# Index scores of a sparse attention: one whole pass and paired half-height matmuls in place of two whole passes

## The chip, the core and the metric

The kernel runs on one core of a Trainium2 chip. The metric is the device time of one execution in microseconds. TensorE (PE) multiplies matrices: each matmul has a weight load of its own (PEld) that can run ahead of it, and sums into one of eight banks of PSUM. ScalarE (ACT), VectorE (DVE) and GpSimd (POOL) work on tiles, and nearly all transfers are issued by SyncE's queue (SP), in its order.

## The reference, cut to what matters

A transformer block on 2048 tokens of width 1024: a first projection, an RWKV-7 branch, a branch of sparse attention, gates, output projections and a norm. The sparse attention chooses for each query its 256 best keys by an index score, and this score is what the change touches:

```python
qi = qi.reshape(B, S, IDX_HEADS, IDX_HEAD_DIM)          # 8 heads of 64
s_idx = jax.nn.relu(jnp.einsum('bqhd,bsd->bqhs', qi_b, ki))
score = jnp.einsum('bqh,bqhs->bqs', wi_b, s_idx).astype(jnp.float32)
score = jnp.where(causal[None], score, -jnp.inf)
_, sel = lax.top_k(score, topk)                         # topk = 256
```

All heads share one key `ki` of 64 numbers a token. Since a choice hangs on the scores, they are computed with operands split in two: a number is the sum of a "hi" part, rounded to the type float32r that TensorE multiplies in one pass, and a "lo" part, the rest.

## The kernel before, in words

`gemm_index` (lines 277 to 299) projects the index keys and queries for all tokens. `split_out` makes the hi and lo tiles of a projected tile ("eo" tiles, a pool of four); the keys go to the DRAM tensor `KIH` (hi and lo), the queries through `stacked` (lines 269 to 275) to `QIS`, where each head has 128 rows: 64 rows of hi and under them 64 of lo. That takes four DMAs of 128 KB for each of 16 projected tiles.

`select` (lines 372 to 496) works on blocks of 128 queries, blocks 2 to 15, in five groups of two or three blocks. For each block a tile `st` of 128 x 8 x 128 is loaded from `QIS` (line 412). The keys lie in SBUF in two tiles: `M[0]` holds the hi part twice, once in each half of the 128 rows, and `M[1]` the lo part twice. Keys up to the end of the block are taken in chunks of up to 512. For each chunk and each of 8 heads, two matmuls of 128 rows sum into a PSUM tile "ixs" (lines 418 and 419): the first gives hi by hi and lo by hi, the second hi by lo and lo by lo. ScalarE takes the relu into a tile "re" (line 421, three buffers), and VectorE adds it, weighted by the head, to the block's scores (line 425 or 427). After a group's scores come passes that seek a threshold (lines 440 to 467) and the mask (488 to 496).

```python
p = ps.tile([128, 512], FT, name="ixs")
T.matmul(p[:, :kn], st[:, h], M[0][:, k0:k0 + kn], start=True, stop=False)
T.matmul(p[:, :kn], st[:, h], M[1][:, k0:k0 + kn], start=False, stop=True)
r = w.tile([128, 512], FT, name="re", bufs=3)
A.activation(r[:, :kn], p[:, :kn], AF.Relu)
```

The pool of "ixs" tiles has six PSUM banks; the two others belong to the projection GEMM (tile "g", line 251), which goes on during the selection: `gemm_half` projects tokens 0 to 1023 for all other columns, 24 matmuls of 512 columns a tile. Its weights are loaded at line 230 and split at lines 236 and 237, and its results are stored from "eo" tiles at lines 340 and 349. A scheduler puts every engine's instructions in order beforehand, by a simulated timeline and by priorities (`band`): the selection has 20000 and the first half's projection 40000, and the lower number goes first where both are ready. After that come the second half's projection in 256-column matmuls, the RWKV-7 stage, the attention and the output projections.

In the RWKV-7 stage there are matmuls over fewer than 128 rows, which the prediction uses: in `rwkv_pass`, line 653 is a matmul over all rows, line 654 one over rows 64 to 127 and line 669 one over 40 rows from row 0, all of 512 columns in float32r.

Of the kernel before, what the change touches and what calls it, by code (L numbers as in the profile page):

```python
# [36 lines left out]
TB = 512  # L37
# [8 lines left out]
# first columns of the projections  # L46
# [5 lines left out]
class Block:  # L52
# [19 lines left out]
    def move(self, dst, src, q=None):  # L72
        """a DMA of float32r words as they are"""
        f = [a.bitcast(FT) if a.dtype == FR else a for a in (dst, src)]
        return (q or self.nc.sync).dma_start(f[0], f[1])
# [4 lines left out]
    # ---------------------------------------------------------------- constants  # L80
    def consts(self):
# [6 lines left out]
        # scratch in DRAM  # L88
        self.QIS = d.tile([8, 128, S], FR, name="qis")
# [22 lines left out]
    # ---------------------------------------------------------------- start: modulation, norm, h^T  # L112
    def start(self):
# [59 lines left out]
        # the last third of the modulation is for the end  # L173
# [9 lines left out]
        # bias by distance; beyond the last bucket's start it is constant and drops out of the softmax  # L183
# [12 lines left out]
    def ada(self, w, cT, j, ahead):  # L196
        """a third of the modulation, partial sums by partition"""
# [15 lines left out]
    # ---------------------------------------------------------------- the projection GEMM  # L213
    @contextmanager
    def urgent(self):
        """what frees or feeds the tensor engine goes before all else"""
        p = self.tc.cur_priority
        self.tc.cur_priority = self.hot
        yield
        self.hot = self.tc.cur_priority  # L220
        self.tc.cur_priority = p
# [33 lines left out]
    def split_out(self, p, scale=None, rows=128):  # L255
        """FR hi and lo of a PSUM tile."""
# [20 lines left out]
    def gemm_index(self):  # L277
# [5 lines left out]
        for tb in range(NTB):  # L283
# [11 lines left out]
            self.stacked(self.QIS, self.unit(qi, tb), 0, tb)  # L295
        for m in range(1, 4):
            wt = self.weights(C_QI + m * 128, 128)
            for tb in range(NTB):
                self.stacked(self.QIS, self.unit(wt, tb), m, tb)

    def gemm_half(self, tbs, kinds):
# [13 lines left out]
        # at the turn of the halves, a block of tokens serves two columns at a time  # L315
# [55 lines left out]
    # ---------------------------------------------------------------- index scores and the selection  # L371
    def select(self):
        """For each query the mask of its TOPK best keys (ties go to the lower index).

        A threshold is sought by the secant method on the count of scores at or above it, until the count is
        at most eight short of TOPK; the missing ones are then the largest below the threshold. Where the
        search has not ended so, a branch finds the TOPK-th largest value bit by bit.
        """
# [3 lines left out]
        with ExitStack() as ctx:  # L382
            k1 = self.pool("ix1", 1, side="right", ctx=ctx)
            w = self.pool("ixw", 2, side="right", ctx=ctx)
            ps = self.pool("ixp", 6, PSUM, ctx=ctx)
            M = [k1.tile([128, S], FR, name=f"kim{i}") for i in range(2)]
            for i in range(2):
                for r in range(2):
                    self.move(M[i][r * 64:r * 64 + 64], self.KIH[i])
# [8 lines left out]
            for grp in self.groups:  # L398
# [9 lines left out]
                for g, qb in enumerate(grp):  # L408
                    n, n1 = 128 * (qb + 1), 128 * qb
                    st = w.tile([128, 8, 128], FR, name="st")  # L410
                    self.move(st, self.QIS[:, :, qb * 128:(qb + 1) * 128].rearrange("h p q -> p h q"))
                    sco = w.tile([128, S], FT, name="sc", bufs=6)
                    sc.append(sco)
                    for k0 in range(0, n, 512):
                        kn = min(512, n - k0)
                        for h in range(8):
                            p = ps.tile([128, 512], FT, name="ixs")
                            T.matmul(p[:, :kn], st[:, h], M[0][:, k0:k0 + kn], start=True, stop=False)  # L418
                            T.matmul(p[:, :kn], st[:, h], M[1][:, k0:k0 + kn], start=False, stop=True)
# [9 lines left out]
                    # a first guess from mean and mean deviation of the keys that all rows see  # L429
# [10 lines left out]
                for it in range(self.passes):  # L440
                    if it:
                        # next threshold: a step of nothing once the count is near enough
# [15 lines left out]
                    for g, qb in enumerate(grp):  # L458
                        n = 128 * (qb + 1)
                        tg, cg = t[:, g:g + 1], cnt[:, g:g + 1]  # L460
                        if qb in self.on_act and it < self.passes - 1:
                            # with Sign a score equal to the threshold counts half: good enough to go on
# [5 lines left out]
                # rows that found their threshold  # L468
# [29 lines left out]
    def select_bits(self, grp, sc, hs, t, cnt, y, eq, w):  # L498
        """The selection for any scores: the TOPK-th largest value bit by bit, ties by prefix sums.

        Leaves 1 for the selected and 0 for the others as scores, and their threshold."""
# [24 lines left out]
    # ---------------------------------------------------------------- RWKV-7, chunks of 64  # L526
    def rwkv_open(self, ctx):
# [23 lines left out]
        # the small second factors: hi twice, and lo  # L551
# [48 lines left out]
    def parts(self, pool, t):  # L600
        """FR hi and lo of a tile"""
# [115 lines left out]
    def rwkv_inv(self, tb):  # L717
        """inverses of the unit triangular 32-blocks, one block a partition"""
# [23 lines left out]
    def rwkv_chain(self, tb):  # L742
# [8 lines left out]
        for c in range(8):  # L751
# [15 lines left out]
            # off-diagonal block of the inverse  # L767
# [51 lines left out]
    def chain_out(self, tb, half, yt, yvar):  # L819
        """group norm and bonus of half a block, with features on partitions"""  # L820
# [21 lines left out]
    # ---------------------------------------------------------------- keys and values of all heads  # L842
# [42 lines left out]
    # ---------------------------------------------------------------- attention over the selected keys  # L885
    def attention(self):
        nc, tc, x, d = self.nc, self.tc, self.x, self.d
        V, A, T, G, DMA = nc.vector, nc.scalar, nc.tensor, nc.gpsimd, nc.sync
        with ExitStack() as ctx:
# [7 lines left out]
            for h in range(8):  # L897
# [18 lines left out]
                for j in range(NQB // 2):  # L916
                    L = []
                    for qb in (2 * j, 2 * j + 1):
                        if h == 0:
                            # masks  # L920
# [66 lines left out]
    # ---------------------------------------------------------------- gates, output projections, last norm  # L987
    def split_weights(self, W, k1, w, names, eng, wide=D, **kw):
        """FR hi and lo of a matrix"""
# [15 lines left out]
    def gated(self, w, ps, fb, br, li=None, at=None, lb="lb"):  # L1005
        """a branch times silu of its gate, hi and lo"""
# [351 lines left out]
```

## Time and profile before

| | us |
|---|---|
| median of 3 runs | 2612.31 |
| lowest and highest run | 2610.18 and 2612.83 |
| span of the profiled execution | 2605.7 |
| TensorE busy in it | 2449.8 |
| VectorE busy in it | 1750.5 |

The span goes from the first to the last instruction of one profiled execution; what lies around it is not in the trace, and no separate time of that execution is listed. The matmuls' ends are modelled, so the distance from one matmul's start to the next one's says more than a duration. "Idle before" names what an engine waited for; "issue" means that the profile shows nothing.

### The profile page before, as it was taken

The page shows a single profiled execution, that of the slowest core. Times are in us where ns is not written, and L with a number is a line of the kernel's source. Part 1 is how long each engine was busy: PE and PEld are TensorE (multiplying, and loading weights), DVE is VectorE, ACT ScalarE, POOL GpSimd, SP SyncE. Part 2 cuts the span into 40 slices and gives each one's busy share as a digit, 9 for nine tenths or more (in the row PEclk, how much of TensorE's full clock was granted, in tenths as well). Part 3 has the DMA queues.
Part 4 walks back from the last instruction along what each step waited for, and adds up shares of the span by engine and source line. Part 5 has one row for each costly group of instructions (what it writes and reads, how often), then busy time and mean ns, then how long its engine had stood idle before and what let it go on. Part 6 is the DMA issues. An engine that isn't in the chain of part 4 may idle for free. (4 is left out here: it accounts for less than half of the span.)

```text
span 2605.7 us, 45357 instructions
## 1 busy us (share of the span) xinstructions
PE 2449.8 (94%) x16776; PEld 2153.8 (83%) x16776; DVE 1750.5 (67%) x3509; ACT 1229.8 (47%) x2136; POOL 868.2 (33%) x707
## 2 busy tenths in 40 slices
PE   4899999989899999899999999999989999999998
PEld 3687777868677899689898888988978999988887
DVE  6615888798988355774956947533468888877443
ACT  4315636446344423324334233343367888865332
POOL 2311131241323333223233322131155545645342
PEclk9999999999999999899999999999999999999999
DMA  7754222522233756568677669977763334145442
GB/s 245 271 149 127 77 85 73 131 77 88 84 103 102 243 162 202 147 192 234 179 219 204 187 189 284 293 233 189 239 199 116 91 88 118 45 152 195 147 150 77
DMA packets 423499, 415.69 MB, mean 160 GB/s; under 512 B 80010, under 2 KB 339890, under 8 KB 418404
## 3 DMA queue, kind: packets, MB, share of 16 engines
q1 hardware_dynamic: 422692, 404.33, 51.7%
q0 software_dynamic: 576, 8.39, 0.8%
q8 instruction: 132, 2.16, 0.4%
q14 instruction: 99, 0.81, 0.1%
HBM read 254.04 MB, written 160.15 MB: 159 GB/s over the span
## 5 line engine op out<-in xcount | busy, mean ns | idle before, releaser
L251 PE MATMUL g<-hh,whi 128*128 128x256 f32 (+1 forms) x2176 | 726.9, 334 | 14.8 <-DVE eo L265 4.5
L251 PE MATMUL g<-hl,whi 128*128 128x256 f32 (+1 forms) x2176 | 722.5, 332 | 3.9 <-POOL hl L169 2.4
L251 PE MATMUL g<-hh,wlo 128*128 128x256 f32 (+1 forms) x2176 | 721.0, 331 | 1.2 <-POOL wlo L237 1.2
L251 PEld LDWEIGHTS g<-hh,whi 128*128 128x128 f32 x2176 | 421.4, 194 | 63.8 <-issue 5.7
L251 PEld LDWEIGHTS g<-hl,whi 128*128 128x128 f32 x2176 | 421.0, 193 | 47.6 <-issue 3.9
L251 PEld LDWEIGHTS g<-hh,wlo 128*128 128x128 f32 x2176 | 420.7, 193 | 42.7 <-issue 3.9
L237 POOL TENSOR_TENSOR wlo<-wraw,whi 128x1024 fp32r<-128x1024 f32 (+1 forms) x89 | 216.9, 2437 | 629.4 <-ACT whi L236 583.0
L421 ACT ACTIVATE re<-ixs 128x512 f32<-128x512 f32 (+3 forms) x304 | 158.9, 548 | 176.1 <-DVE sc L427 109.8
L427 DVE SCALAR_TENSOR_TENSOR sc<-re,wi,sc 128x512 f32<-128x512 f32 (+3 forms) x266 | 222.6, 842 | 21.7 <-ACT re L421 6.5
L236 ACT CAST whi<-wraw 128x1024 fp32r<-128x1024 f32 (+1 forms) x89 | 92.8, 1042 | 175.1 <-PE g L251 131.0
L957 PE MATMUL pt<-ident,lt 128*128 128x128 f32 x1088 | 168.2, 276 | 6.4 <-ACT tp L963 3.5
L947 ACT ACTIVATE lt<-lt,nm 128x128 f32<-128x128 f32 (+15 forms) x128 | 154.7, 1211 | 14.2 <-DVE nm L946 14.1
L943 DVE CUSTOM_DVE_ANT_0 lt<-lg,mask 128x512 f32<-128x512 f32 (+3 forms) x256 | 147.4, 590 | 15.9 <-PE lg L941 7.5
L974 PE MATMUL yv<-ph,vp 128*128 128x256 f32 (+1 forms) x576 | 151.5, 285 | 6.7 <-ACT yl L978 4.7
L968 DVE TENSOR_TENSOR pl<-pt,ph 128x512 fp32r<-128x512 f32 (+1 forms) x216 | 139.1, 657 | 25.7 <-ACT ph L967 24.6
L974 PE MATMUL yv<-pl,vp 128*128 128x256 f32 x576 | 152.4, 300 | 2.0 <-POOL pl L965 2.0
L418 PE MATMUL ixs<-kim,st 128*128 128x512 f32 (+3 forms) x304 | 117.3, 387 | 28.7 <-ACT re L421 24.8
L940 PE MATMUL lg<-m,sq 128*128 128x256 f32 (+3 forms) x384 | 137.2, 366 | 5.0 <-DVE cm L943 4.1
L957 PEld LDWEIGHTS pt<-ident,lt 128*128 128x128 f32 x1088 | 125.9, 141 | 15.6 <-ACT tp L963 4.5
L941 PE MATMUL lg<-m,sq 128*128 128x256 f32 (+3 forms) x384 | 127.4, 337 | 0.0
L733 DVE TENSOR_TENSOR prd<-tm,ln 128x1 f32<-128x1 f32 (+30 forms) x124 | 113.3, 914 | 20.5 <-DMA pk<-pj 14.6
L967 ACT CAST ph<-pt 128x512 fp32r<-128x512 f32 (+1 forms) x216 | 115.9, 565 | 19.7 <-PE pt L957 13.7
(347 smaller groups left out, 5391.4 us busy)
## 6 DMA issues: line engine op xcount, KB each, us to landing
wraw<-in_w_in_dram SPq DMA_DIRECT2D x88, 512.0 KB
gg<-eo SPq DMA_DIRECT2D x64, 256.0 KB
gmd<-gt SPq DMA_DIRECT2D x64, 256.0 KB
gmc<-gmd SPq DMA_DIRECT2D x32, 512.0 KB
g<-gg SPq DMA_DIRECT2D x64, 256.0 KB
m<-ks SPq DMA_DIRECT2D x32, 512.0 KB
pj<-eo SPq DMA_DIRECT2D x52, 256.0 KB
x<-in_ada_w_dram SPq DMA_DIRECT2D x24, 512.0 KB
```

Source lines behind the costliest of these rows:

```text
L237: nc.gpsimd.tensor_tensor(lo[:, :, :n], raw[:, :, :n], hi[:, :, :n].bitcast(FT), op=OP.subtract)
L251: T.matmul(p[:, s], a[:, k], b[:, k, s], start=n == 0, stop=n == 3 * KD - 1)
L418: T.matmul(p[:, :kn], st[:, h], M[0][:, k0:k0 + kn], start=True, stop=False)
L421: A.activation(r[:, :kn], p[:, :kn], AF.Relu)
L427: V.scalar_tensor_tensor(o, r[:, :kn], wi, o, op0=OP.mult, op1=OP.add)
L940: T.matmul(p[:, :kn], sq[:, qb * 128:(qb + 1) * 128], m1[:, k0:k1_], start=True, stop=False)
L941: T.matmul(p[:, :kn], sq[:, qb * 128:(qb + 1) * 128], m2[:, k0:k1_], start=False, stop=True)
L943: V.tensor_tensor_reduce(lt[:, k0:k1_], p[:, :kn], mk, 1.0, -3.0e38, OP.add, OP.max, cm[:, i:i + 1])
L947: ex = A.activation(lt[:, :n], lt[:, :n], AF.Exp, bias=nm, accum_out=lsum[:, qb, h:h + 1])
L957: T.transpose(p[:, o:o + 128], L[i][:, kt * 128:(kt + 1) * 128], self.ident)
L968: V.tensor_tensor(pl[:, :n], p[:, :n], ph[:, :n].bitcast(FT), op=OP.subtract)
L974: T.matmul(yv[:, qs], vp[:, kt, :], b[:, o:o + nn], start=kt == 0 and i == 0, stop=kt == last and i == 1, skip_group_check=True)
```

## The change

The query's hi and lo parts go to two DRAM tensors, `QIH` (8 heads of 64 rows) and `QIL` (4 pairs of heads, 128 rows), in two DMAs of 256 KB for each projected tile. `M[0]` now holds the keys' hi part in rows 0 to 63 and the lo part in rows 64 to 127; of `M[1]` only rows 64 to 127 are filled, with the hi part. For each block `st` holds the query's hi part twice (two loads), and a tile `lo` with one buffer holds the lo parts of two heads in its two row halves. Heads are taken four at a time: four matmuls of 128 rows give hi by hi and hi by lo, then four matmuls of 64 rows, in the lower and the upper row half by turns, add lo by hi to the same four PSUM tiles. `manual_schedule` keeps TensorE to this order within a group of four; what else TensorE does in between is left to the scheduler. The product of lo by lo is no longer computed. Relu and weighted sum stay as they are.

```diff
-        self.QIS = d.tile([8, 128, S], FR, name="qis")
+        self.QIH = d.tile([8, 64, S], FR, name="qih")
+        self.QIL = d.tile([4, 128, S], FR, name="qil")
...
-            self.stacked(self.QIS, self.unit(qi, tb), 0, tb)
+            self.index_out(self.unit(qi, tb), 0, tb)
...
+    def index_out(self, p, m, tb):
+        hi, lo = self.split_out(p)
+        s = slice(tb * TB, (tb + 1) * TB)
+        self.move(self.QIH[2 * m:2 * m + 2, :, s].rearrange("h p t -> (h p) t"), hi)
+        self.move(self.QIL[m, :, s], lo)
...
-            for i in range(2):
-                for r in range(2):
-                    self.move(M[i][r * 64:r * 64 + 64], self.KIH[i])
+            for r in range(2):
+                self.move(M[0][r * 64:r * 64 + 64], self.KIH[r])
+            self.move(M[1][64:128], self.KIH[0])
...
                     st = w.tile([128, 8, 128], FR, name="st")
-                    self.move(st, self.QIS[:, :, qb * 128:(qb + 1) * 128].rearrange("h p q -> p h q"))
+                    lo = w.tile([128, 4, 128], FR, name="stl", bufs=1)
+                    for r in range(2):
+                        self.move(st[r * 64:r * 64 + 64],
+                                  self.QIH[:, :, qb * 128:(qb + 1) * 128].rearrange("h p q -> p h q"))
+                    self.move(lo, self.QIL[:, :, qb * 128:(qb + 1) * 128].rearrange("m p q -> p m q"))
...
                         for h in range(8):
-                            p = ps.tile([128, 512], FT, name="ixs")
-                            T.matmul(p[:, :kn], st[:, h], M[0][:, k0:k0 + kn], start=True, stop=False)
-                            T.matmul(p[:, :kn], st[:, h], M[1][:, k0:k0 + kn], start=False, stop=True)
+                            if h % 4 == 0:
+                                with tc.manual_schedule(engines={mybir.EngineType.PE}):
+                                    pp = [ps.tile([128, 512], FT, name="ixs") for _ in range(4)]
+                                    for i, p in enumerate(pp):
+                                        T.matmul(p[:, :kn], st[:, h + i], M[0][:, k0:k0 + kn], start=True, stop=False)
+                                    for i, p in enumerate(pp):
+                                        r_ = slice(i % 2 * 64, i % 2 * 64 + 64)
+                                        T.matmul(p[:, :kn], lo[r_, (h + i) // 2], M[i % 2][r_, k0:k0 + kn],
+                                                 start=False, stop=True)
+                            p = pp[h % 4]
```

## Rows read from the trace of the kernel before

**Rows 1.** The page: busy time with share of the span, and PE's busy tenths.
```profile
PE 2449.8 (94%) x16776; PEld 2153.8 (83%) x16776; DVE 1750.5 (67%) x3509; ACT 1229.8 (47%) x2136; POOL 868.2 (33%) x707
...
PE   4899999989899999899999999999989999999998
```

**Rows 2.** Windows: length, busy of PE, PEld, DVE, ACT, POOL; clock, DMA share, GB/s.
```profile
217.00:806.00 589.00, 553.60 (x2368) 443.07 (x2369) 508.23 (x935) 308.46 (x527) 146.49 (x47) 0.97 0.30 88
806.00:851.00 45.00, 45.00 (x201) 36.95 (x200) 31.50 (x130) 15.67 (x30) 14.33 (x13) 1.00 0.44 139
```

**Rows 3.** Windows of the tile "ixs" alone: PE, PEld, DVE, ACT.
```profile
217.00:806.00 589.00, 168.23 (x616) 113.57 (x616) 0.59 (x4) 158.57 (x303) 0.97 0.30 88
```

**Rows 4.** Timeline at the end of the first half: start, us, engine, line.
```profile
850.84 0.28 PE L251 MATMUL g<-hh,whi 128*128 128x256 f32 x1
...
854.09 0.81 DVE L494 MATCH_REPLACE8 y<-m,y 128x640 f32<-128x640 f32 x1
```

**Rows 5.** The page's costliest groups: the weighted sum; busy us, mean ns.
```profile
L427 DVE SCALAR_TENSOR_TENSOR sc<-re,wi,sc 128x512 f32<-128x512 f32 (+3 forms) x266 | 222.6, 842 | 21.7 <-ACT re L421 6.5
```

**Rows 6.** Timeline of PE: one head's two index matmuls, at 512 and at 128 keys.
```profile
230.05 0.39 PE L418 MATMUL ixs<-kim,st 128*128 128x512 f32 x1
230.28 0.40 PE L419 MATMUL ixs<-kim,st 128*128 128x512 f32 x1
230.51 0.40 PE L418 MATMUL ixs<-kim,st 128*128 128x512 f32 x1
...
409.96 0.22 PE L418 MATMUL ixs<-kim,st 128*128 128x128 f32 x1
410.02 0.28 PE L419 MATMUL ixs<-kim,st 128*128 128x128 f32 x1
```

**Rows 7.** Waits from 217 to 852 us: total us, times, longest us.
```profile
ACT re L421 <- DVE sc L427: 109.8, 118, 4.2
...
PEld ixs L418 <- ACT re L421: 37.8, 32, 3.8
...
PE ixs L418 <- ACT re L421: 24.8, 15, 3.3
```

**Rows 8.** Timeline: matmuls and weight loads around half-height matmuls; idle in brackets.
```profile
897.57 0.40 PE L653 MATMUL pg<-sa,a2s 128*128 128x512 f32 x1
897.89 0.18 PEld L654 LDWEIGHTS pg<-sa,wa2l 64*128 64x128 f32 x1 [0.25 <-issue]
897.90 0.50 PE L654 MATMUL pg<-sa,wa2l 64*128 64x512 f32 x1
...
898.33 0.39 PE L251 MATMUL g<-hh,wlo 128*128 128x256 f32 x1
...
898.55 0.28 PE L251 MATMUL g<-hh,whi 128*128 128x256 f32 x1
...
1332.84 0.50 PE L654 MATMUL pg<-sa,wa2l 64*128 64x512 f32 x1
...
1332.84 0.50 PE L669 MATMUL pg<-nrs,oneht 40*128 40x512 f32 x1
...
1333.27 0.38 PE L251 MATMUL g<-hh,wlo 128*128 128x256 f32 x1
```

**Rows 9.** DMA issues of the tile "qis": ns least/median/largest, first to last start.
```profile
L75 SPq DMA_DIRECT2D qis<-eo x64: 445/587/1229, 72.8 to 202.4; - x64
L75 SPq DMA_DIRECT2D st<-qis x14: 370/377/1701, 211.6 to 775.5; - x14
```

**Rows 10.** Timeline: a block's first load and the first index matmul.
```profile
211.63 2.13 SPq L75 DMA_DIRECT2D st<-qis  x2
...
217.34 0.76 PE L418 MATMUL ixs<-kim,st 128*128 128x512 f32 x1 [3.01 <-DMA st<-qis]
```

**Rows 11.** Waits: of ACT from 60 to 217 us, of SP from 217 to 852.
```profile
ACT eo L261 <- DMA qis<-eo: 6.9, 1, 6.9
...
SPq L349 <- ACT eo L347: 234.2, 41, 12.9
```

More of the change, by code (lines that the diff above doesn't have):

```diff
@@ L298, in gemm_index @@
             for tb in range(NTB):
-                self.stacked(self.QIS, self.unit(wt, tb), m, tb)
+                self.index_out(self.unit(wt, tb), m, tb)
+    def index_out(self, p, m, tb):
[3 more added lines that the diff above has]
+        self.move(self.QIL[m, :, s], lo)
     def gemm_half(self, tbs, kinds):
@@ L415, in select @@
                         kn = min(512, n - k0)
+                        pp = []
                         for h in range(8):
-                            p = ps.tile([128, 512], FT, name="ixs")
-                            T.matmul(p[:, :kn], st[:, h], M[0][:, k0:k0 + kn], start=True, stop=False)
-                            T.matmul(p[:, :kn], st[:, h], M[1][:, k0:k0 + kn], start=False, stop=True)
+                            if h % 4 == 0:
[8 more added lines that the diff above has]
+                            p = pp[h % 4]
                             r = w.tile([128, 512], FT, name="re", bufs=3)
```

## The prediction

> **What bounds the kernel now.** I read the page's busy shares and slices first, then the stretch around the change in windows, then the waits, then TensorE's matmuls one by one. TensorE (PE) is the bound: it is busy for 94% of the span, and its row of slices hardly leaves 8 or 9 after the first tenth, while VectorE (DVE) has 67% and ScalarE (ACT) 47% [rows 1]. The index scores run from 217 to 806 us. In that stretch 616 of the 2368 matmuls are theirs; the other 1752 are of the projection GEMM, which fills in between [rows 2, 3]. After the last of them TensorE does almost nothing but projection matmuls, 201 in 45 us without a gap, until tokens 0 to 1023 are projected and the 256-column matmuls of the second half begin at 850.84; VectorE still selects at 854.09 [rows 2, 4]. So a microsecond of TensorE time gained or lost before 806 moves what follows by about as much, since the later slices are dense too.
>
> Within the stretch TensorE is not full. The chain is TensorE, relu on ACT, weighted sum on DVE: DVE takes 842 ns a head [rows 5], while a head's two 512-column matmuls start 0.23 us apart and take 0.46 [rows 6]. So index matmuls wait for a PSUM bank: weight loads of line 418 waited 37.8 us for ACT in 32 waits, and its matmuls 24.8 us in 15; ACT itself waited 109.8 us for DVE [rows 7].
>
> **The change, part by part.** For each block of 128 queries and chunk of keys the eight heads become two groups of four. There are 304 heads with chunk, so 76 groups: 56 of 512 keys, 8 of 384, 6 of 256 and 6 of 128, by the loops (blocks 2 to 15, chunks of 512).
>
> *The pairs.* Of the eight matmuls of four heads, four stay at full height and four become half height, in two pairs. Whether two halves overlap is shown in this trace: line 654 (rows 64 to 127) and line 669 (40 rows from row 0), both of 512 columns, start together at 1332.84, and the next full matmul starts at 1333.27, 0.43 us later. One half matmul alone is also followed after 0.43 us (897.90 to 898.33) [rows 8]. So the second of a pair is free, and two pairs cost two matmuls in place of four. That saves two starts a group, 2 x 0.23 = 0.46 us at 512 columns [rows 6], and by their columns 0.345 at 384 and 0.23 at 256; at 128 the second matmul of a head cost only 0.06 us [rows 6], and I take no gain. 56 x 0.46 + 8 x 0.345 + 6 x 0.23 = **-29.9 us**.
>
> *The change of height.* At 897.57 a full 512-column matmul starts, the half one follows after 0.33 us instead of 0.23, the next full one 0.43 us later, and the one after that after 0.22, where 256 columns need half of 0.23; the half one's weight load sat idle 0.25 us for "issue" instead of running ahead [rows 8]. From 897.57 to 898.55 that is 0.98 us, where 0.23 + 0.23 + 0.12 = 0.58 would do: 0.40 us for one trip to half height and back. Each group makes one trip if nothing comes between its four halves: 76 x 0.40 = **+30.4 us**. Where TensorE waits anyway as a trip ends, its price falls. Projection matmuls between the halves would make two trips of one, but all four halves can run once the fourth full one has a bank, so I take one.
>
> The Trainium skill, page "TensorEngine Tiling (Array Packing)", states under "Key Properties" that changing the tiling mode drains TensorE, and under "Theoretical Speedup" that a dimension of at most 64 gives up to 2x. By the second alone the sum would be about -28 us; by the first, which the page gives no price for and rows 8 agree with at 0.40 us a trip, the two cancel.
>
> *The loads of a block.* The hi tile now comes in two loads and the lo tile in a third: 42 issues in place of 14, 28 x 0.377 = 10.6 us more on the SP queue [rows 9], and 14 x 256 KB more. SP spends 234.2 us waiting for ACT on line 349 alone [rows 11], and DMA stands at a share of 0.30 there [rows 2]: nothing, at most the 10.6. Queued behind a load that waits are the stores of the projection's tiles (lines 340 and 349) and the weight loads of line 230, and behind the stores the four "eo" tiles that ACT writes.
>
> *A new wait.* The lo tile has one buffer. Its load for the next block is held until the last half matmul of this one, and the next block's first half matmuls wait for it on TensorE, with all projection matmuls queued behind. This can happen at the 9 turns inside the five groups of query blocks; between groups the selection passes leave time. Cover: the next block's four full matmuls need four banks, which DVE frees at 842 ns each, 3.4 us [rows 5]. A block's load took from its issue at 211.63 to TensorE's start at 217.34, 5.7 us; from the end of the 2.13 us in which two such loads were issued it is 3.6 [rows 10]. Bounds: 9 x 0.2 = 1.8 and 9 x 2.3 = 20.7. The lo tile is half of what that load moved, so I take the lower end, **+1.8 us**.
>
> *The stores of the query projections.* 64 stores of 128 KB become 32 of 256 KB: 32 x 0.587 = 18.8 us less on SP between 72 and 202 us [rows 9]. One wait of ACT for such a store was 6.9 us [rows 11], no other is in that list: 0, at best -6.9. One key load of four goes, before the first scores: 0. The lo by lo product, which is dropped, shared its matmuls with others and had no time of its own.
>
> *The order.* Four results now come at once, and six banks hold one group and a half. DVE has two finished banks and three relu tiles in hand, about 5 x 0.84 us, against some 3 us from a group's first bank to its first result. So 0. But the scheduler lays out the whole program anew, and waits can move both ways; as an estimate I allow a fifth of the 62.6 us of rows 7, 12 us, to either side.
>
> Sum: -29.9 + 30.4 + 1.8 = +2.3 us on the profiled execution's span of 2605.7 us, hence 2608.0. The median of the runs lies 6.6 us above that span; the forecast is 2612.3 + 2.3 = 2614.6 us.
>
> **The rivals.** *Faster: the trips fall into waits.* In 47 waits TensorE stood still for a bank before line 418 [rows 7]. Where the next instruction after a group is a full matmul that has to wait, the way back, 0.30 of the 0.40 us, costs nothing. For half of the 76 groups that is -11.4 us, 2603; for all of them -22.8, 2592; were both ways free, 2584. For it: 62.6 us of such waits. Against it: the scheduler fills the time that its own timeline leaves open with projection matmuls, and these pay the trip. (Free both ways is what the Trainium skill's up-to-2x on the same page comes to; rows 8 show a price.)
>
> *Slower: the single lo buffer.* TensorE stands at each turn of a block for the full 5.7 us less 3.4, and the price is 20.7 in place of 1.8: 2633. It decides once a load takes over 3.4 us from the last half matmul. For it: the first load of a block did keep TensorE waiting 3.01 us [rows 10]. Against it: a late TensorE gives DVE time to catch up, so part of this wait takes the place of those in rows 7.
>
> *The change doesn't do what it says.* If the halves, which here add to a bank that a full one has just written, ran one after another, the -29.9 is gone: 2644. The pair of rows 8 speaks against it.
>
> **How the numbers follow.** A measurement here can tell about 0.2% (5.2 us) from no change. The cancelling case has 0.37; its own range is 2608 to 2621, with 0.27 of it within the 5.2 us, 0.08 above, 0.02 below. Trips in waits have 0.30 (0.27 faster, 0.03 same; free both ways is 0.02 of it), the lo buffer 0.23 (0.20 slower, 0.03 same), no overlap 0.05 (slower), a rearrangement elsewhere 0.05 (0.03 faster, 0.02 slower). That gives faster 0.32, same 0.33, slower 0.35. The range leaves out no overlap and the ends of the others: 2592 to 2636.
>
> **What would show it.** In the changed profile the halves should stand in two pairs with starts a few ns apart, about 0.32 us from pair to pair; a full matmul should follow the last pair after 0.43 us; the weight loads at both turns should show "issue" idle; and TensorE's last projection matmul of the first half should start near 851. Half matmuls 0.23 us apart would prove the third rival. Waits of half matmuls for a DMA into the lo tile, of over a microsecond at 9 places, would prove the second; waits for "re" well below 62.6 us with the first half ending before 840, the first. A changed time with the stretch up to 851 as it was would make all of this wrong.

## The result and the profile after

| | before | after |
|---|---|---|
| median of the runs side by side, us (4 of each) | 2611.24 | 2675.02 |
| lowest and highest, us | 2608.82 and 2612.83 | 2665.85 and 2679.96 |
| span of the profiled execution, us | 2605.7 | 2678.2 |
| first index matmul, us | 217.3 | 216.1 |
| last index matmul, us | 805.6 | 909.1 |
| projection of the first half over, us | 850.8 | 818.2 |
| selection's last MATCH_REPLACE8, us | 854.1 | 966.1 |
| RWKV-7 stage's first matmul, us | 892.9 | 986.4 |
| last matmul of that stage's chain (`pp<-uv,gmc`), us | 1830.5 | 1918.8 |

The ratio is 1.0244, with an interval from 1.0218 to 1.0269: 64 us slower, and 39 us above the upper end of the range. The page's lines that answer to [rows 1]:

```profile
PE 2489.7 (93%) x16776; PEld 2155.8 (80%) x16776; DVE 1735.1 (65%) x3509; ACT 1221.3 (46%) x2132; POOL 868.5 (32%) x707
PE   4899999999999998989999999878989999989998
PEclk9999999999999999999999996768989999999999
```

TensorE looks as full as before until the 24th of 40 slices. Then, from about 1600 us, its busy digits and the clock granted to it drop together. That is where the time shows as lost; what lost it comes before 966. Windows of the same kernel (length, busy of PE, PEld, DVE, ACT and POOL with counts, clock, DMA share, GB/s), the third row for the tile "ixs" alone:

```profile
217.00:806.00 589.00, 564.06 (x2446) 426.75 (x2445) 445.21 (x753) 280.37 (x471) 143.55 (x47) 0.97 0.34 97
1600.00:1800.00 200.00, 168.38 (x1249) 139.35 (x1247) 113.52 (x191) 58.22 (x104) 29.27 (x40) 0.69 0.73 221
217.00:806.00 589.00, 136.67 (x535) 67.73 (x533) 0.44 (x3) 131.26 (x264) 0.97 0.34 97
```

Against [rows 2, 3]: up to 806 TensorE started 2446 matmuls in place of 2368, but 535 on the tile "ixs", the index scores, in place of 616. Its other matmuls went from 1752 to 1911. TensorE was given more projection and fewer scores, so the projection ended 33 us earlier and the selection 112 us later.

The waits from 217 to 900 us (total us, times, longest us):

```profile
ACT re L442 <- PE ixs L438: 108.1, 43, 7.0
ACT re L442 <- DVE sc L448: 62.2, 52, 4.2
PEld ixs L435 <- ACT re L442: 31.5, 26, 3.4
PE ixs L435 <- ACT re L442: 22.0, 19, 3.0
```

The list before (217 to 852 us) has the wait of ACT for TensorE too:

```profile
ACT re L421 <- PE ixs L419: 31.8, 24, 4.5
```

TensorE's waits for a bank are much as they were: 22.0 us of its matmuls and 31.5 of its weight loads, against 24.8 and 37.8 [rows 7]. ACT's wait for scores rose from 31.8 to 108.1 us, and its wait for DVE fell from 109.8 [rows 7] to 62.2. DVE in turn waited 42.1 us for a relu before its weighted sums, against 6.5 [rows 5]:

```profile
L448 DVE SCALAR_TENSOR_TENSOR sc<-re,wi,sc 128x512 f32<-128x512 f32 (+3 forms) x266 | 225.1, 846 | 62.4 <-ACT re L442 42.1
```

The chain of relu and weighted sum, which used to wait mostly for its own end, is now starved by TensorE. A stretch of TensorE's timeline (start, busy us, line) shows how; after the first projection matmul shown (line 252) come 16 more, some 0.23 us apart:

```profile
224.24 0.40 PE L435 MATMUL ixs<-kim,st 128*128 128x512 f32 x1
224.57 0.74 PE L438 MATMUL ixs<-kim,stl 64*128 64x512 f32 x4
225.24 0.74 PE L435 MATMUL ixs<-kim,st 128*128 128x512 f32 x2
225.81 0.39 PE L252 MATMUL g<-hl,whi 128*128 128x512 f32 x1
...
229.69 0.40 PE L435 MATMUL ixs<-kim,st 128*128 128x512 f32 x1
...
230.16 0.40 PE L435 MATMUL ixs<-kim,st 128*128 128x512 f32 x1
230.48 0.74 PE L438 MATMUL ixs<-kim,stl 64*128 64x512 f32 x4
231.15 0.73 PE L435 MATMUL ixs<-kim,st 128*128 128x512 f32 x2
```

ACT and DVE in the same stretch:

```profile
225.10 2.08 ACT L442 ACTIVATE re<-ixs 128x512 f32<-128x512 f32 x4 [3.55 <-PE ixs L438]
231.01 2.07 ACT L442 ACTIVATE re<-ixs 128x512 f32<-128x512 f32 x4 [1.72 <-PE ixs L438]
```

```profile
225.73 3.32 DVE L448 SCALAR_TENSOR_TENSOR sc<-re,wi,sc 128x512 f32<-128x512 f32 x4 [2.61 <-ACT re L442]
```

A group's four results come after its fourth bank. Of six banks two are then left, so the next group gets two full matmuls at 225.24, and its third and fourth need the banks of this group's first two heads. The first relu began at 225.10 and takes 0.52 us, a quarter of the 2.08, so that bank was free near 225.6; the third full matmul starts at 229.69. Between them lie 17 projection matmuls without a gap. No wait of TensorE shows: its order was fixed beforehand, with the projection in between. So the next four heads come after 5.91 us here (225.24 to 231.15), and DVE, which needs 3.32 us for them, is idle for the rest or does other work. Over all 304 heads with chunk, the times from the first to the last index matmul of the five groups of query blocks add up to 474.7 us, before to 374.1: 1.56 us a head in place of 1.23.

### The profile page after: what moved, and what is told of

Its sections match the earlier page's. It is cut to its first block, busy times and chain, and to the rows that moved or that the text cites. A ratio compares the mean times of both kernels' runs of the same rounds, so it can differ in the third digit from the quotient of the medians.

```text
span 2678.2 us, 45432 instructions
## 1 busy us (share of the span) xinstructions
PE 2489.7 (93%) x16776; PEld 2155.8 (80%) x16776; DVE 1735.1 (65%) x3509; ACT 1221.3 (46%) x2132; POOL 868.5 (32%) x707
## 4 chain that ended last, share of the span: by engine, by line
PE 38%; DVE 12%; DMA 6%; issue 4%; ACT 2%; POOL 2%; SPq 1%; POOLq 0%; ACTq 0%; DVEq 0%
PE g L252 7%; PE fo L1198 5%; PE br L1113 5%; PE yv L995 4%; DVE prd L754 3%; PE pt L978 3%; PE lg L961 2%; PE lg L962 2%; PE pg L719 2%; DVE tm L756 2%; PE zu L811 1%; DMA g<-gg 1%; PE hp L815 1%; PE pp L802 1%; PE pp L822 1%
## 5 line engine op out<-in xcount | busy, mean ns | idle before, releaser
L238 POOL TENSOR_TENSOR wlo<-wraw,whi 128x1024 fp32r<-128x1024 f32 (+1 forms) x89 | 226.2, 2541 | 652.5 <-ACT whi L237 612.9
L448 DVE SCALAR_TENSOR_TENSOR sc<-re,wi,sc 128x512 f32<-128x512 f32 (+3 forms) x266 | 225.1, 846 | 62.4 <-ACT re L442 42.1
L442 ACT ACTIVATE re<-ixs 128x512 f32<-128x512 f32 (+3 forms) x304 | 150.4, 546 | 210.6 <-PE ixs L438 108.1
L435 PE MATMUL ixs<-kim,st 128*128 128x512 f32 (+3 forms) x304 | 112.4, 406 | 26.7 <-ACT re L442 23.2
```

What stands on the lines that cost most here:

```text
L238: nc.gpsimd.tensor_tensor(lo[:, :, :n], raw[:, :, :n], hi[:, :, :n].bitcast(FT), op=OP.subtract)
L448: V.scalar_tensor_tensor(o, r[:, :kn], wi, o, op0=OP.mult, op1=OP.add)
```

## The experiments

The table gives what all of them showed; times in us, the ratio with its interval against runs of before on the same chip. "Shift" is against the trace of before, for the end of the first half's projection and for the selection's last MATCH_REPLACE8. Before as the first line has no shift.

| kernel | median | before | ratio | last index matmul | projection shift | selection shift |
|---|---|---|---|---|---|---|
| before | 2611.24 | | | 805.6 | | |
| after | 2675.02 | 2611.24 | 1.0244 (1.0218 to 1.0269) | 909.1 | -32.7 | +112.0 |
| e1_full4 | 2654.96 | 2610.40 | 1.0162 (1.0144 to 1.0181) | 903.2 | -25.2 | +105.7 |
| e5_banks4 | 2633.12 | 2610.40 | 1.0075 (1.0048 to 1.0102) | 871.3 | -28.8 | +71.9 |
| e7_full2 | 2610.23 | 2606.23 | 1.0017 (1.0001 to 1.0034) | 808.8 | -3.2 | +9.8 |
| e2_pairs2 | 2619.53 | 2610.40 | 1.0040 (1.0025 to 1.0054) | 838.3 | +0.3 | +38.1 |
| e6_pairs2_lo2 | 2622.29 | 2606.23 | 1.0066 (1.0044 to 1.0089) | 820.0 | +7.1 | +19.8 |
| e8_single | 2656.28 | 2606.23 | 1.0206 (1.0173 to 1.0239) | 872.2 | +45.8 | +72.3 |
| e3_free4 | 2664.46 | 2610.40 | 1.0198 (1.0171 to 1.0225) | 873.9 | +47.0 | +74.3 |
| e9_after_lo2 | 2651.88 | 2606.23 | 1.0183 (1.0159 to 1.0207) | 890.0 | -29.5 | +93.7 |
| e10_hs3 | 2669.03 | 2609.71 | 1.0233 (1.0205 to 1.0261) | 910.4 | -29.9 | +112.4 |
| e12_after_again | 2672.48 | 2609.71 | 1.0254 (1.0222 to 1.0286) | 911.9 | -30.2 | +114.6 |
| e11_full3 | 2596.40 | 2609.71 | 0.9949 (0.9925 to 0.9973) | 818.7 | -14.6 | +20.7 |
| e13_full3_again | 2600.59 | 2608.82 | 0.9973 (0.9950 to 0.9996) | 817.7 | -15.5 | +19.1 |

The theory: the order, with results in fours on six banks, makes the scores late, and their lateness costs the time. The rivals: the trips to half height, the single buffer of the lo tile. The change drops the lo by lo product; so do e2, e3, e6, e8, e9, e10 and e12, while e1, e5, e7, e11 and e13 compute what the kernel before computes.

**The order of four without half height (e1).** Edit, to the kernel before:

```diff
-                            p = ps.tile([128, 512], FT, name="ixs")
-                            T.matmul(p[:, :kn], st[:, h], M[0][:, k0:k0 + kn], start=True, stop=False)
-                            T.matmul(p[:, :kn], st[:, h], M[1][:, k0:k0 + kn], start=False, stop=True)
+                            if h % 4 == 0:
+                                with tc.manual_schedule(engines={mybir.EngineType.PE}):
+                                    pp = [ps.tile([128, 512], FT, name="ixs") for _ in range(4)]
+                                    for i, p in enumerate(pp):
+                                        T.matmul(p[:, :kn], st[:, h + i], M[0][:, k0:k0 + kn], start=True, stop=False)
+                                    for i, p in enumerate(pp):
+                                        T.matmul(p[:, :kn], st[:, h + i], M[1][:, k0:k0 + kn], start=False, stop=True)
+                            p = pp[h % 4]
```

> The kernel before with the order of four alone: four full matmuls with the keys' hi part, then four full ones with the lo part, held to this order. No half height, no pairs, the loads of before. Order theory (a group's results come only after its fourth full matmul has a bank, and six banks hold one group and a half, so VectorE starves and the selection ends late): the last index matmul starts near 909 us as in the changed kernel (805.6 before), and the time is 1.02 to 1.03 of before, 2660 to 2690 us. Rival, half height (trips between heights, or the loads of the lo tile, make the index scores slow): the last index matmul starts within 15 us of 805.6 and the time is within 0.5% of before.

It gives 45 of the change's 64 us (1.0162), where I expected 1.02 or more, and nearly the whole lateness of the scores: 903.2 against 909.1. None of its index matmuls has half height, and no lo tile exists. Its timeline of TensorE, and its wait of ACT from 217 to 900 us:

```profile
228.35 0.39 PE L421 MATMUL ixs<-kim,st 128*128 128x512 f32 x1
228.58 1.09 PE L423 MATMUL ixs<-kim,st 128*128 128x512 f32 x4
229.51 0.63 PE L421 MATMUL ixs<-kim,st 128*128 128x512 f32 x2
229.98 0.40 PE L251 MATMUL g<-hh,whi 128*128 128x512 f32 x1
...
235.47 0.63 PE L421 MATMUL ixs<-kim,st 128*128 128x512 f32 x2
```

```profile
ACT re L426 <- PE ixs L423: 100.1, 43, 5.1
```

The same pattern with nearly the same period, 5.96 us (229.51 to 235.47), and the same starved ACT. The order alone makes the scores late.

**Fewer banks, heads one by one (e5).** Edit, to the kernel before:

```diff
-            ps = self.pool("ixp", 6, PSUM, ctx=ctx)
+            ps = self.pool("ixp", 4, PSUM, ctx=ctx)
```

> The kernel before with four PSUM banks for the index scores in place of six; no other edit. Order theory (results in flight set the pace of the selection): the five index stretches, 374 us in sum before, grow to 400 to 450 us at unchanged TensorE work, the selection ends later and the time is 0.5 to 2% above before. Rival (TensorE's own work sets the time, which is unchanged here): within 0.3% of before.

```profile
ACT re L421 <- PE ixs L419: 92.6, 78, 4.4
```

With two banks fewer and the order of before, ACT starves for scores as well (92.6 us, the wait above in its own trace), the scores end 66 us late and the kernel is 0.75% slower. The five index stretches add up to 449.1 us, at the upper end of what was expected. So a shortage of banks by itself starves the consumers too. The loss is less than e1's, though four banks are fewer than six; that single heads hand their banks back one by one fits this, but was not shown.

**The order of two without half height (e7), and of three (e11, e13).** As e1, with groups of two, and with groups of three, three and two:

```diff
-                            if h % 4 == 0:
+                            if h % 3 == 0:
-                                    pp = [ps.tile([128, 512], FT, name="ixs") for _ in range(4)]
+                                    pp = [ps.tile([128, 512], FT, name="ixs") for _ in range(min(3, 8 - h))]
-                            p = pp[h % 4]
+                            p = pp[h % 3]
```

> The kernel before with two heads at a time, all at full height: two full matmuls with the hi keys, then two with the lo keys, held to this order. It is the two-head version without pairs and trips. Trip theory (152 trips cost TensorE 61 us and pairs give back 30): without them the first half's projection ends some 10 to 30 us earlier than the two-head version's 851 us, at a last index matmul of 815 to 845 us; time 0.995 to 1.003 of before. Rival (order of two is what costs, the trips fall into waits): as the two-head version, 1.003 to 1.006, and the first half ends within 8 us of 851.

> The kernel before with groups of three, three and two heads, all at full height and held to the order of hi keys first. Six banks hold two groups of three. Order theory: between the order of two (1.0017, last index matmul 808.8 us) and the order of four (1.0162, 903.2 us): last index matmul 825 to 875 us, time 1.003 to 1.012 of before. Rival (four is a case of its own, by the number of banks that it leaves over): as the order of two, 1.003 or less, last index matmul under 820 us.

> The groups of three at full height once more, in five rounds. Theory of two bounds (the time follows the later of the first half's projection and of the selection less some 50 us of cover): projection 15 us earlier, selection 20 us later, hence 8 to 18 us below before, 0.993 to 0.997. Rival (the first comparison was a difference between chips' runs): 0.998 to 1.002.

Groups of two leave the scores nearly where they were (808.8) and the time 0.17% above before, with an interval from 1.0001 to 1.0034. The first half's projection ends only 3.5 us before that of e2 (below), where I expected 10 to 30. Six banks hold three such groups, or two groups of three; they hold no two of four. With three I expected scores between 825 and 875 and a slower kernel, and that was wrong: they end at 818.7, the first half's projection 15 us earlier than before (836.21, below), and the kernel is 0.5% faster, the best of all here. Run once more (e13) it was 0.9973, just outside what I then expected, and again below 1.

```profile
836.21 0.28 PE L251 MATMUL g<-hh,whi 128*128 128x256 f32 x1
```

**Half height with fewer heads a trip (e2, e6, e8, e3).** e2 is the change with groups of two (two full matmuls, one pair), e6 the same with two lo buffers, made room for by three in place of four tiles "hs" of the comparisons, e8 head by head (one full matmul, one half), and e3 the change without the line of `manual_schedule`:

```diff
-                            if h % 4 == 0:
+                            if h % 2 == 0:
-                                    pp = [ps.tile([128, 512], FT, name="ixs") for _ in range(4)]
+                                    pp = [ps.tile([128, 512], FT, name="ixs") for _ in range(2)]
-                            p = pp[h % 4]
+                            p = pp[h % 2]
```

> The changed kernel with two heads at a time: two full matmuls, then one pair of half-height ones; 152 trips in place of 76. Order theory: six banks hold three groups, the last index matmul goes back to 805 to 845 us, and what is left is TensorE's price of 152 x 0.40 - 30 = +31 us at most: 2612 to 2645 us. Rival, half height: twice the trips, so the last index matmul is later than 909 us and the time above 2675 us.

> The kernel with two heads at a time, and two buffers for the lo tile (room is made by three in place of four buffers for the tiles that hold the counts' comparisons). Theory, lo buffer: at the nine turns of a block the halves wait for the next lo tile; without that the last index matmul moves from 838 us to 825 or earlier and the time from 1.004 to 0.995 to 1.001 of before. Rival, the buffer is hidden (what is left above before is the trips' price): the time stays at 1.002 to 1.007 and the last index matmul within 10 us of 838.

> The changed kernel head by head, as before the change: one full matmul and then one half-height matmul, no pairs, no fixed order. Each head makes a trip of its own, 304 in place of 76. Trip theory at 0.40 us: TensorE pays 122 us, of which up to 62.6 can fall into its waits for a bank; the first half's projection ends between 885 and 970 us in place of 850.8, and the time is 1.015 to 1.045 of before. Rival (what costs is the order of four alone, trips are hidden): the first half ends within 15 us of 850.8 and the time is within 0.5% of before.

> The changed kernel without the fixed order on TensorE; four heads are still traced together. Order theory: where a full matmul waits for a bank, halves that are ready go first, more trips but earlier results: last index matmul between 820 and 890 us, 2620 to 2665 us. Rival, half height: more trips and broken pairs make it slower than the changed kernel, over 2675 us.

The expectations say 152 trips for two heads at a time and 304 for one. In the traces the runs of half-height index matmuls with nothing between them number 135 in e2, 151 in e6, 257 in e8 and 242 in e3, since the scheduler let some halves follow each other; after has its 76. With many trips TensorE's own time is what the kernel pays for. e6 against e7, which has the same order at full height, ends the first half's projection 10.4 us later and costs 0.5% more. In e8 it ends 45.8 us later than before, and the kernel is 50 us slower. e8's timeline shows trips one by one:

```profile
240.23 0.39 PE L433 MATMUL ixs<-kim,st 128*128 128x512 f32 x1
240.55 0.49 PE L434 MATMUL ixs<-kim,stl 64*128 64x512 f32 x1
240.97 0.49 PE L433 MATMUL ixs<-kim,st 128*128 128x512 f32 x1
241.40 0.49 PE L434 MATMUL ixs<-kim,stl 64*128 64x512 f32 x1
241.82 0.50 PE L252 MATMUL g<-hh,wlo 128*128 128x512 f32 x1
...
896.64 0.28 PE L252 MATMUL g<-hh,whi 128*128 128x256 f32 x1
```

Full to half 0.32 and 0.43, half to full 0.42 and 0.42 us, where matmuls of one height stand 0.23 apart [rows 6]. Two heads take 1.59 us in place of 0.92, so 0.33 us a trip here. 257 such trips would be 85 us, as an estimate. The projection ended 46 us later, and TensorE's idle time from 217 us to that end fell from 35 us before (633.8 less 598.4 busy) to 7 (679.6 less 672.3): 28 us of the trips' price fell into time that was idle anyway, and the two together, 74 us, come near the estimate. e3 shows what the line of `manual_schedule` is for: without it the scheduler put most half matmuls right behind their full ones, and 39 pairs were left of 152. Its time is that of e8 within the intervals.

**The lo tile's buffers (e9, e10, e12).** e9 is the change with two lo buffers and three "hs" tiles; e10 has only the three "hs" tiles; e12 is the change once more:

```diff
-                    lo = w.tile([128, 4, 128], FR, name="stl", bufs=1)
+                    lo = w.tile([128, 4, 128], FR, name="stl", bufs=2)
...
-                hs = [w.tile([128, S], BF, name="hs", bufs=4) for _ in grp]
+                hs = [w.tile([128, S], BF, name="hs", bufs=3) for _ in grp]
```

> The changed kernel with two buffers for the lo tile (and three in place of four for the comparisons' tiles). Theory, lo buffer: up to 20.7 us of the 64 go, time 1.014 to 1.019 of before, near that of the order of four at full height (1.016). Order theory: the buffer's wait hides behind the order of four; time within 0.4% of the changed kernel, 1.020 to 1.028, last index matmul within 10 us of 909.

> The changed kernel with three in place of four buffers for the comparisons' tiles, and the lo tile's one buffer kept: the control for the run with two lo buffers. Theory, the lo buffer made that run faster: this one stays at 1.021 to 1.028 of before, last index matmul 900 to 918 us. Rival, the room taken from the comparisons' tiles (or a rearranged schedule) did it: 1.016 to 1.021, last index matmul near 890 us.

> The changed kernel once more, beside its version with three comparison buffers on the same chip: 1.021 to 1.027 of before if the first comparison holds; nothing else is told apart by it.

The interval of e9 (up to 1.0207) lies below that of the change (from 1.0218), of e12 (from 1.0222) and touches that of e10 (from 1.0205). The "hs" tiles alone change nothing that the intervals tell apart (1.0233 against 1.0244 and 1.0254). So the single buffer costs about 0.5 to 0.7%, some 15 us; the selection ends 18.7 us earlier in e9 than in e10. It is seen in the order: at the first turn of a block, in the change,

```profile
265.20 0.86 PE L435 MATMUL ixs<-kim,st 128*128 128x512 f32 x3
...
266.36 0.39 PE L435 MATMUL ixs<-kim,st 128*128 128x512 f32 x1
...
270.36 0.73 PE L438 MATMUL ixs<-kim,stl 64*128 64x512 f32 x4
```

and in e9:

```profile
268.33 0.62 PE L435 MATMUL ixs<-kim,st 128*128 128x512 f32 x2
268.88 0.73 PE L438 MATMUL ixs<-kim,stl 64*128 64x512 f32 x4
```

In the change the last of the four full matmuls starts at 266.36, and their halves come at 270.36, with 16 projection matmuls between. The load of this block's lo tile starts only at 262.67 there. In e9 the halves follow the last pair of full ones after 0.55 us. e2 and e6 show no such gain: e6's scores end at 820.0 and e2's at 838.3, as expected, but e6's time was expected at 0.995 to 1.001 and came out at 1.0066, no better than e2's within the intervals. By the rule of the next section a selection this little late costs nothing by itself.

## Why the prediction was wrong, point by point

**The step that failed is "The order".** It held that DVE "has two finished banks and three relu tiles in hand, about 5 x 0.84 us, against some 3 us from a group's first bank to its first result. So 0." The timeline shows that nothing is in hand: a group of four leaves two banks, and the next group cannot finish until it has two more. In the stretch shown DVE got four heads in 5.9 us for its 3.3 us of work. By e1 this step alone is worth +45 us (ratio 1.0162), and the 12 us allowed to either side were far too few. Those 12 us were taken from 62.6 us of waits, which add up two rows of one engine, matmuls and weight loads; TensorE's matmul row was idle for 589 - 553.60 = 35.4 us in that stretch [rows 2]. The account compared how long DVE's stock lasts with how long TensorE needs, as if TensorE would turn to the scores at once; in the trace it does 17 projection matmuls first. That the scheduler lays out the program anew was named as a risk, with a chance of 0.02 for slower.

**The frame failed with it.** "A microsecond of TensorE time gained or lost before 806 moves what follows by about as much" is half of the rule. Here TensorE time was gained (the first half's projection ended at 818.18, not 850.84 [rows 4]), and the kernel lost 64 us. The other half is the selection: the RWKV-7 stage starts behind it. In the chain of work that ended last in after, the stage's first load comes right behind the store of the selection's last mask (start, us):

```profile
966.05 0.82 DVE y L515
...
969.40 1.81 DMA mask<-mk
...
971.34 2.46 DMA pk<-in_w_dram
```

In before this load starts at 877.81, 2.2 us behind the start of the last mask's store at 875.63. The stage's first matmul comes 15.1 us behind that load in both. It is 20.3 us behind the last MATCH_REPLACE8 in after (986.4), 38.8 us behind it in before (892.9), and 19.7 to 29.1 us behind it in the other runs. First and last start of that line, before and after:

```profile
L631 PE MATMUL pg<-kk,oneh x16: 388/394/628, 892.9 to 1421.7; 128*8 128x512 f32 x16
```

```profile
L652 PE MATMUL pg<-kk,oneh x16: 393/394/493, 986.4 to 1527.0; 128*8 128x512 f32 x16
```

Over the runs the change of the median is near the larger of two numbers, the projection's shift and the selection's shift less some 50 us, where 50 is fitted to the runs before e13:

| kernel | selection shift - 50 | projection shift | measured change of the median |
|---|---|---|---|
| after | +62.0 | -32.7 | +63.8 |
| e10_hs3 | +62.4 | -29.9 | +59.3 |
| e12_after_again | +64.6 | -30.2 | +62.8 |
| e1_full4 | +55.7 | -25.2 | +44.6 |
| e9_after_lo2 | +43.7 | -29.5 | +45.7 |
| e5_banks4 | +21.9 | -28.8 | +22.7 |
| e3_free4 | +24.3 | +47.0 | +54.1 |
| e8_single | +22.3 | +45.8 | +50.1 |
| e6_pairs2_lo2 | -30.2 | +7.1 | +16.1 |
| e2_pairs2 | -11.9 | +0.3 | +9.1 |
| e7_full2 | -40.2 | -3.2 | +4.0 |
| e11_full3 | -29.3 | -14.6 | -13.3 |
| e13_full3_again | -30.9 | -15.5 | -8.2 |

It misses by 11 us at most (e1) and by 7 to 9 us in e2, e3, e6, e7 and e13, so it orders the large changes and says little of the small ones. Where the selection is the late one, the loss is seen later. The windows of before, and of e1 and e5, of the same length and columns as above:

```profile
1600.00:1800.00 200.00, 194.61 (x1892) 180.00 (x1890) 103.91 (x153) 75.11 (x130) 46.82 (x45) 0.97 0.81 252
```

```profile
1600.00:1800.00 200.00, 174.29 (x1441) 145.97 (x1442) 117.32 (x200) 71.87 (x128) 34.34 (x47) 0.77 0.83 249
```

```profile
1600.00:1800.00 200.00, 176.79 (x1538) 153.02 (x1538) 122.14 (x206) 72.81 (x127) 39.90 (x47) 0.85 0.85 256
```

In e8, late through TensorE itself, TensorE stays full there:

```profile
1600.00:1800.00 200.00, 195.95 (x1851) 180.37 (x1850) 112.96 (x184) 75.48 (x134) 43.66 (x45) 0.97 0.85 261
```

What is missing after 1600 is filler: 1249 matmuls start in the 200 us of after, 1892 in before. The projection of both halves is the same work in all runs. First and last start of one of its three groups of matmuls, before and after:

```profile
L251 PE MATMUL g<-hh,wlo x2176: 274/283/723, 45.6 to 1747.8; 128*128 128x256 f32 x122, 128*128 128x512 f32 x76
```

```profile
L252 PE MATMUL g<-hh,wlo x2176: 274/283/632, 44.7 to 1618.4; 128*128 128x256 f32 x122, 128*128 128x512 f32 x76
```

In after the projection runs out 129 us earlier. Of these 33 were there at 818 already; the rest came while the late RWKV-7 stage left TensorE to the projection. The end of that stage's chain, whose small matmuls depend on each other, has then no projection beside it for 300 us (1618.4 to 1918.8), in before for 83 (1747.8 to 1830.5). By the traces it is 203 us in e5, 229 in e9, 257 in e1, 286 and 287 in e12 and e10, and 84 to 122 in all the others, e8 and e3 among them (87 and 95). Which part of the fitted 50 us is cover at the stage's start (18.5 us by the distances above) and which comes from projection work repaid later was not separated.

**"The pairs" and "The change of height" held.** In after the four halves take 0.67 us (224.57 to 225.24), and a window of the trace that ends 0.05 us after the first half's start already holds two of them. One full matmul, the halves and the two full ones after them take 1.57 us (224.24 to 225.81), in e1 the same seven matmuls, with four full ones for the halves, 1.63 (228.35 to 229.98): 0.06 us saved a group, where -0.46 + 0.40 was forecast. So the two do cancel within a tenth of a us a group, and e9, which has no late lo tile, stands beside e1 at 1.0183 against 1.0162, its interval from 1.0159. The Trainium skill, page "TensorEngine Tiling (Array Packing)", "Key Properties", has TensorE drain where the tiling mode changes; these traces agree, with 0.33 us a trip in e8 and, by the 1.57 us less five starts of 0.233, 0.40 in after.

**"A new wait" had the right bounds and the wrong end.** Bounds 1.8 to 20.7 us, taken 1.8; measured some 15. That 15 lies within the bounds is partly luck, for it hardly came about as a wait. The cover was counted as four banks' worth of DVE, 3.4 us, against the transfer. The order was laid out with the halves late, which costs TensorE nothing: projection matmuls stand in between. At the turn shown the halves start 4.0 us behind the last full one's start (270.36 less 266.36). The rival built on it (2633) had the place right, but with two buffers 45.7 of the 63.8 us stay. Put together, the 2.44% are 1.62% of the order (e1), about 0.6% of the lo buffer, and a rest of 0.2%, within the intervals, for half height.

**"The stores" and "The loads of a block"** took nothing that can be seen: the first index matmul starts at 216.1, before at 217.3.

The 62.6 us named for the first rival count TensorE twice: its matmuls waited 24.8 us for a bank [rows 7], hardly more than the 22.8 us that this rival needed at its best price for one way.

Of what was to show it: halves in pairs, yes; "issue" at the turns, yes (the weight loads of the halves sat idle 23.3 us in 69 places); the first half's end near 851, no. The waits for "re" at 53.5 us didn't fall "well below 62.6", and the first half ended before 840 for a reason the first rival didn't have: TensorE was on the wrong work.

**What stays open:** why the scheduler sets the third matmul of a group 17 projection matmuls late, when its bank was free 4 us before. Its reckoning of banks was not taken apart, and the order of four was not run with more than six banks. Why three heads a group beat single heads was not traced beyond the earlier end of the projection.

## What to carry to other kernels

When results share a ring of PSUM banks, count how many groups of them the ring holds. Here six banks held groups of two and of three without harm and let the consumers run dry with groups of four. That the ring holds two groups is not enough by itself: single heads on four banks starved the consumers too (e5). Where filler is laid out beforehand, a starved consumer shows as its own wait, not as a gap of the full engine, so a full TensorE does not prove that the right work is on it. To amortise a change of tile height over more matmuls, count first the banks that the larger group holds: here a group of four saved 0.06 us of TensorE's time and brought its scores 1.3 us later (474.7 less 374.1 us over 76 groups).

## What the runs showed of the hardware

Four half-height matmuls of 512 columns on two row halves take 0.67 us together, in two pairs, right behind full-height ones into the same banks, where four full ones took 0.93 (228.58 to 229.51 in e1). A trip to half height and back costs about the same whether one half matmul (0.33 us in e8) or four (0.40) are in it. What I had not expected at all is that a late stage pays twice, in idle time and in clock. Windows of after (columns as above) in the RWKV-7 stage:

```profile
1600.00:1620.00 20.00, 20.00 (x192) 17.41 (x191) 7.01 (x12) 8.42 (x14) 4.10 (x6) 1.00 0.56 161
1620.00:1640.00 20.00, 19.28 (x132) 16.44 (x130) 7.66 (x15) 3.03 (x6) 4.36 (x5) 0.56 0.50 152
1680.00:1700.00 20.00, 18.56 (x143) 16.75 (x142) 7.25 (x28) 4.01 (x8) 1.53 (x3) 0.50 0.61 153
1705.00:1710.00 5.00, 5.00 (x21) 4.11 (x20) 4.76 (x11) 1.09 (x2) 0.30 (x1) 0.50 0.50 153
```

and TensorE's timeline in the last of them:

```profile
1708.40 0.63 PE L889 MATMUL p<-lat,w_ukh 128*128 128x512 f32 x1
1708.83 0.63 PE L889 MATMUL p<-lat,w_ukl 128*128 128x512 f32 x1
```

Up to 1620 TensorE is busy throughout and granted 1.00, the 2.4 GHz level. Its last projection matmul starts at 1618.4. In the 20 us from 1620 the mean is 0.56, though TensorE is idle for only 0.72 us there: it now runs the RWKV-7 stage's matmuls, most of them small, 132 in place of 192 in all. From 1680 to 1700 it is at 0.50, the 1.2 GHz level, and at 0.50 full matmuls of 512 columns, filler too, stand 0.43 us apart (1708.40 to 1708.83) in place of 0.23. So once the projection has run out, TensorE waits for the chain (31.6 us of the 200 from 1600, in before 5.4), and the work between the waits is slower as well. What made the clock fall is not shown beyond this sequence. Over the 200 us from 1600 the mean was 0.69 in after, 0.77 in e1 and 0.85 in e5, and 0.97 in before and e8, where TensorE had projection to fill in until 1747.8 and 1791.2. How much of the 64 us is clock and how much is idle time was not separated.
